# First column pair of a SwiGLU block: operand sums by halves, the order of casts and bank copies, and the buffer of the second pair's weights

## The chip, the cores and the metric

The kernel runs on one core of one Trainium2 chip. The metric is the device time of one execution in microseconds (us), as the median of several runs. Engines are named as the profile names them: PE multiplies matrices (PEld loads its weights), DVE and ACT do elementwise work, POOL a few small things, SP issues DMAs. Each engine takes its instructions strictly in the order in which the program issues them, and semaphores hold an instruction until what it needs is there.

## The reference, cut to what matters

One residual block over a sequence of 1024 rows and 1024 features: a mixer (gated DeltaNet heads beside a short convolution), then SwiGLU with 2816 hidden columns, then a last RMSNorm. Everything is float32.

```python
for l in range(DEPTH):
    shift1, scale1, gate1, shift2, scale2, gate2 = jnp.split(mod, 6, axis=-1)
    h = rms_norm(x, norm1_w[l]) * (1.0 + scale1) + shift1
    x = x + gate1 * hybrid_mixer(h, ...)
    h = rms_norm(x, norm2_w[l]) * (1.0 + scale2) + shift2
    x = x + gate2 * swiglu(h, w_gate[l], w_up[l], w_down[l])
return rms_norm(x, norm_f_w)

def swiglu(h, w_gate, w_up, w_down):
    return (jax.nn.silu(h @ w_gate) * (h @ w_up)) @ w_down
```

The change lies where the mixer ends and the first two products of SwiGLU, `h @ w_gate` and `h @ w_up`, begin.

## The kernel before

**Stages.** The first 520 us of the profile are the mixer and its output projection. From there to 944 us PE makes `h @ w_gate` and `h @ w_up` (matmuls into tiles named `acc`), then `@ w_down` (tiles named `dn`).

**Precision.** Every operand is held as two fp32r parts: a high part `hi`, the cast of the value (on ACT), and a low part `lo`, the value less `hi` (on DVE). One product of 128x512 is three matmuls, hi·hi, hi·lo and lo·hi (line 1859). So each operand tile costs one ACT instruction and one DVE instruction, the second waiting for the first.

**Tiling.** The 2816 hidden columns are taken in 11 pairs `p` of 256 columns. For a pair, gate (q = 0) and up (q = 1) are each a product of 2x2 blocks done with seven block products instead of eight (the Winograd form of Strassen's method). `STEPS` (line 44) lists the seven steps by bank, weight operand, activation operand, and whether the bank is begun anew:

```python
STEPS = (("X", "A11", "B11", True), ("Y", "A12", "B21", True), ("X", "S2", "T2", False), ("Z", "S1", "T1", True),
         ("X", "S3", "T3", False), ("Z", "S4", "B22", False), ("X", "A22", "T4", False))
```

The A operands are blocks of the weights, S1 to S4 sums of them: S1 = A21 + A22, S2 = S1 - A11, S3 = A11 - A21, S4 = A12 - S2. The B operands are blocks of the transposed activations, T1 to T4 sums of those. `run(p, s, q_)` issues step `s`: 12 matmuls for each q, 24 for both. Before a bank is added to further, its running value is taken out: `keep` copies both q of it into a `cc` tile (ACT), `close` adds it to one (DVE).

**The first pair.** For p = 0 the T operands and B22 don't exist yet. They are made once, between the steps of the first pair, in an order written out by hand at the end of the function (from line 2094), while the steps of all later pairs come from the loop `block(p, s)`. The helpers there: `t_split(n, banks)` transposes four tiles on PE into four PSUM banks (`tr`); `t_turned(n)` makes the hi and lo parts from these banks and, for T2, then copies the four banks into the `raw` tiles `tm[k]` with ACT; `t_sums` and `t_parts` make T3 and T4 from tiles in SBUF; `part(n, q)` makes hi and lo of a weight operand; `W[0].sum_n(n)` makes a weight sum, for p = 0 as two instructions, one for each q. The four transposes of T1 use the same four banks as those of T2, so they come after the copies of T2's banks.

**Weights.** `Weights(p).load(half)` issues two DMAs of 512 KB (gate and up) into one R tile of a pool with two R buffers. That pool is opened on the room of the x tiles, after these have been read for the last time: the first buffer lies over the tiles x 0 and x 1, the second over x 2 and x 3. The last readers of these are the four instructions of `t_sums("T4")`, one for each x tile.

**Names in rows.** `hl`: hi and lo of a weight operand; `S`: a weight sum; `T` or `h` with `tr`: hi and lo of T2, T1 or B22; `raw<-tr`: the copies of T2's banks; `raw<-x,raw`: T4's sums; `x<-raw,db,x`: T3's sums; `R<-R`: S3; `R<-R,S`: S4. All rows of this part of the program have line L89 (PE) or L90 (the others), which are the lines of a helper.

Of the kernel before, what the change touches and what calls it, by code (L numbers as in the profile page):

```python
# [9 lines left out]
F32 = mybir.dt.float32  # L10
F32R = mybir.dt.float32r
BF16 = mybir.dt.bfloat16
AF = mybir.ActivationFunctionType
ALU = mybir.AluOpType
# [3 lines left out]
P = 128  # L18
# [33 lines left out]
def kernel(  # L52
# [67 lines left out]
    class Banks:  # L120
# [3 lines left out]
        def get(self, name="ps"):  # L124
            b = self.ids[self.i % len(self.ids)]
            self.i += 1
            return psp.tile([P, HT], F32, name=nm(name), tag=f"b{b}")
# [78 lines left out]
    def split(raw, hi, lo, eng, hi_eng=ACT):  # L206
        cpy(hi_eng, hi, raw)
        eng.tensor_tensor(lo, raw, hi.bitcast(F32), ALU.subtract)
# [334 lines left out]
    b2c = cst.tile([P, KB], F32, name="b2c", tag="b2c")  # L543
# [1251 lines left out]
    def t_split(n, banks):  # L1795
        for k in range(4):
            def get(k=k):
                if n == "T1":
                    return h_slot(k, 1)
                if n == "B22":  # L1800
                    return h_slot(k + 4, 1)
                return mp.tile([P, 2, HT], F32R, name=nm(n), tag=f"{n}_{k}", bufs=1)
            c0 = k * P + (HT if n == "B22" else 0)
            srcs = [tm[i][:, k * P:(k + 1) * P] if n == "T2" else
                    x2n[i + (4 if n == "B22" else 0)][:, c0:c0 + P] for i in range(4)]
            ps = bank_tile(banks[k], "tr")
            for i, src in enumerate(srcs):
                pe("pe", PE.transpose(ps[:, i * P:(i + 1) * P], src, ident))
            t_ps[n, k] = ps, get

    def t_turned(n):
        for k in range(4):
            ps, get = t_ps[n, k]
            B[n][k] = dst = get()
            hi, lo = dst[:, 0, :], dst[:, 1, :]
            if n == "T1":
                split(ps, hi, lo, DVE)
            else:
                col = b2c[:, 4 + k:5 + k]
                ACT.activation(hi, ps, AF.Identity, bias=col, scale=1.0)  # L1820
                DVE.scalar_tensor_tensor(lo, ps, col, hi.bitcast(F32), ALU.add, ALU.subtract)
        if n == "T2":
            for k in range(4):
                ACT.copy(tm[k], t_ps[n, k][0])

    t_ps = {}

    def t_sums(n):
        for k in range(4):
            if n == "T3":  # L1830
                DVE.scalar_tensor_tensor(kept[k], tm[k], db2[:, k:k + 1], kept[k], ALU.add, ALU.subtract)
            else:
                DVE.tensor_tensor(tm[k], kept[4 + k], tm[k], ALU.subtract)
# [6 lines left out]
    def part(n, q):  # L1840
        W[0].cast(n, q)
        W[0].low(n, q)
# [69 lines left out]
    def close(p, n, b):  # L1912
        for q in (0, 1):
            DVE.tensor_tensor(c[p][n][q], c[p][n][q], bk[p][q][b], ALU.add)
# [43 lines left out]
    def block(p, s):  # L1958
# [17 lines left out]
        elif s == 1:  # L1976
            if w:
                if p < 2:
                    keep(p, "p1", "X")
                w.cast("S1", 0)  # L1980
                w.cast("S1", 1)
            if p > 0:
                o = p - 1
                a11, s1, a21 = c[o]["p1"][0], c[o]["p1"][1], c[o]["u2"][0]
                DVE.tensor_tensor(a11, s1, a11, ALU.subtract)
                DVE.tensor_tensor(a21, c[o]["z5"][1], a11, ALU.subtract)
                store(o, "S2", a11)
                store(o, "S4", a21)
            if w:
                w.low("S1", 0)  # L1990
                w.low("S1", 1)
                w.sum_n("S3")
        elif s == 2:
            if p < 2:
                close(p, "p1", "Y")
            else:
                close_inner(p, "p1")
            w.cast("S3", 0)
            silu(p, "p1")
            w.cast("S3", 1)  # L2000
            w.low("S3", 0)
            w.low("S3", 1)
            act(p, "p1")
            store(p, "A11", c[p]["p1"][0])
            w.sum_n("S4")
        elif s == 3:
            keep(p, "u2", "X")
            w.mat("S4")
            prep_gate(p - 1)
        elif s == 4:  # L2010
            keep(p, "z5", "Z")
            w.mat("A22")
            prep_sums(p - 1)
            if last:
                first_mats(0, "A11", am_scr)
        elif s == 5:
            close(p, "z5", "X")
            if n:
                n.cast("A11", 0)
            silu(p, "z5")  # L2020
            if n:
                n.cast("A11", 1)
                n.low("A11", 0)
                n.low("A11", 1)
            act(p, "z5")
            store(p, "A22", c[p]["z5"][0])
            if last:
                first_mats(1, "B11", None)
        elif s == 6:
            close(p, "u2", "Z")  # L2030
            if n and p:
                n.inner_sums()
                n.inner_cast(0)
            elif n:
                n.cast("A12", 0)
            silu(p, "u2")
            if n and p:
                n.inner_cast(1)
                n.inner_low(0)
                n.inner_low(1)  # L2040
            elif n:
                n.cast("A12", 1)
                n_slot[0] += 2
                n.low("A12", 0)
                n.low("A12", 1)
            act(p, "u2")
            a11, a21, a22, s1, s3 = c[p]["p1"][0], c[p]["u2"][0], c[p]["z5"][0], c[p]["p1"][1], c[p]["u2"][1]
            DVE.tensor_tensor(s1, a21, a22, ALU.add)
            DVE.tensor_tensor(s3, a11, a21, ALU.subtract)
            store(p, "S1", s1)  # L2050
            store(p, "S3", s3)
            if n and p:
                for i in (2, 3):
                    n.inner_cast(i)
                    n.inner_low(i)
            if last:
                first_mats(2, "A12", am_scr)
# [36 lines left out]
    dma(x2_scr[7], x2[7])  # L2094
    run(0, 0)
    run(0, 1, (0,))
    W[0].sum_n("S1")
    W[0].sum_n("S2")
    keep(0, "p1", "X")
    part("S2", 0)  # L2100
    part("S2", 1)
    t_split("T2", (6, 7, 4, 5))
    t_turned("T2")
    part("S1", 0)
    run(0, 1, (1,))
    t_split("T1", (6, 7, 4, 5))
    part("S1", 1)
    t_turned("T1")
    close(0, "p1", "Y")
    run(0, 2)  # L2110
    t_sums("T3")
# [4 lines left out]
    t_parts("T3")  # L2116
    run(0, 3, (0,))
    part("S3", 1)
    t_sums("T4")
    W[0].sum_n("S4")  # L2120
    t_split("B22", (6, 7, 2, 3))
    part("S4", 0)
    t_turned("B22")
    x2_ctx.__exit__(None, None, None)
    xq_ctx = tc.tile_pool(name="xq", bufs=1, side="right", reuse_waits="tile")
    xq = xq_ctx.__enter__()
    W[1] = Weights(1)
    W[1].load(0)
    W[1].load(1)
# [2 lines left out]
    run(0, 4)  # L2132
    part("S4", 1)
    part("A22", 0)
    t_parts("T4")
    part("A22", 1)
    act(0, "p1")
# [244 lines left out]
```

## Time and profile before

| | us |
|---|---|
| median of 3 runs (lowest, highest) | 1160.85 (1160.6, 1161.65) |
| the profiled execution, its own time | 1163.06 |
| its span, from the first to the last instruction | 1161.1 |
| mixer and output projection, to the first `acc` matmul of SwiGLU | 520.2 |
| the first column pair, steps 0 to 6 | 520.2 to 566.9 |
| the other ten pairs | 566.9 to 944 |
| `@ w_down` and the last norm | 944 to 1161 |

The span is the time between the first and last instruction of one profiled execution; its own time has 2 us more around it. A timeline row gives start, length, engine, line, operation, output and inputs with their size, the number of merged instructions, and in brackets the idle time before them with what ended it. A merged row's length runs to the end of its last instruction, and consecutive matmuls overlap, so how long a group took on PE is read from its start to the next group's start.

### The profile page before, as it was taken

To read this page: it belongs to the slowest core of one execution; us is meant where nothing else is said; L and a number is where in the kernel's file an instruction comes from. 1 tells how busy PE (TensorE), PEld (TensorE's weight loads), DVE (VectorE), ACT (ScalarE), POOL (GpSimd) and SP (SyncE) were. 2 spreads that over 40 slices of the span, in tenths; PEclk is the share of its full clock that TensorE was granted. 3 is DMA by queue.
4 is the path that set the end of the run, shared out by engine and by line. 5 is a ranking of instruction groups with operands and counts; after the bars stand their busy time and mean duration, and the time that the engine had idled before them with its cause. 6 is when DMAs were issued, how large, how long until landed. Compare 5 with 4: busy or idle time off the path is not lost.

```text
span 1161.1 us, 16878 instructions
## 1 busy us (share of the span) xinstructions
PE 1149.2 (99%) x5682; PEld 967.1 (83%) x5682; DVE 957.9 (83%) x1807; ACT 571.5 (49%) x1257; POOL 59.5 (5%) x100
## 2 busy tenths in 40 slices
PE   9999999999999999999999999999999999999997
PEld 7888888888888888888788888888888888888886
DVE  7899889899987898668987779777887798688676
ACT  7779633459634552445534443434434465443344
POOL 2110001002101010100000000000000000000002
PEclk9999999999999999999999999999999999999999
DMA  9823455534225455432464456545654599869403
GB/s 360 325 90 103 146 164 152 181 119 148 96 67 172 155 189 172 184 100 63 164 217 148 153 191 217 176 136 179 235 187 142 176 331 392 310 207 339 143 31 145
DMA packets 127542, 209.18 MB, mean 180 GB/s; under 512 B 20576, under 2 KB 45152, under 8 KB 127456
## 3 DMA queue, kind: packets, MB, share of 16 engines
q1 hardware_dynamic: 122080, 204.90, 51.5%
q10 hardware_dynamic: 5376, 3.21, 0.9%
q8 instruction: 45, 0.74, 0.2%
q14 instruction: 41, 0.34, 0.1%
HBM read 153.01 MB, written 55.05 MB: 179 GB/s over the span
## 4 chain that ended last, share of the span: by engine, by line
PE 90%; DVE 4%; ACT 2%; DMA 2%; issue 1%; ACTq 0%; SPq 0%; POOL 0%; DVEq 0%
PE acc L89 33%; PE acc L448 25%; PE dn L89 17%; PE o L448 4%; PE o L89 1%; PE A L448 1%; PE K L448 1%; DMA R<-in_w_up_dram 1%; DVE xo L90 1%; PE ab L448 1%; PE O L448 1%; PE kk L448 1%; DVE x L90 1%; DVE h L90 1%; ACT hl L90 0%
## 5 line engine op out<-in xcount | busy, mean ns | idle before, releaser
L448 PE MATMUL acc<-h,u 128*128 128x512 f32 x1200 | 298.6, 397 | 0.0
L448 PEld LDWEIGHTS acc<-h,u 128*128 128x128 f32 x1200 | 219.4, 188 | 42.4 <-issue 0.5
L89 PE MATMUL acc<-h,hl 128*128 128x512 f32 x576 | 135.3, 390 | 0.9 <-ACT cc L90 0.9
L89 PE MATMUL acc<-T,hl 128*128 128x512 f32 x552 | 130.9, 390 | 0.9 <-DVE cc L90 0.9
L89 PEld LDWEIGHTS acc<-h,hl 128*128 128x128 f32 x576 | 107.3, 188 | 23.2 <-ACT cc L90 1.3
L89 PEld LDWEIGHTS acc<-T,hl 128*128 128x128 f32 x552 | 102.3, 188 | 21.7 <-issue 1.3
L90 DVE TENSOR_TENSOR xo<-xo,dn 128x512 f32<-128x512 f32 x84 | 57.0, 683 | 42.3 <-PE dn L89 34.5
L89 PE MATMUL acc<-h,u 128*128 128x512 f32 (+1 forms) x480 | 91.8, 341 | 0.0
L89 PE MATMUL dn<-h,h 128*128 128x512 f32 x396 | 90.7, 389 | 0.0
L89 PEld LDWEIGHTS acc<-h,u 128*128 128x128 f32 x480 | 78.3, 189 | 11.7
L89 PEld LDWEIGHTS dn<-h,h 128*128 128x128 f32 x396 | 74.3, 188 | 15.4
L448 ACT CAST u<-raw 128x512 fp32r<-128x512 f32 x66 | 40.6, 620 | 63.8 <-PE acc L448 60.4
L90 DVE TENSOR_TENSOR cc<-cc,acc 128x512 f32<-128x512 f32 x66 | 41.4, 645 | 32.6 <-PE acc L89 32.6
L448 DVE TENSOR_TENSOR u<-raw,u 128x512 fp32r<-128x512 f32 x82 | 56.1, 686 | 9.1 <-ACT u L448 8.8
L89 PE MATMUL acc<-T,u 128*128 128x512 f32 x240 | 56.0, 389 | 0.0
L448 DVE SCALAR_TENSOR_TENSOR cv<-pr,cols_a,cv 128x512 f32<-128x512 f32 x72 | 53.4, 747 | 0.9 <-ACT cv L448 0.5
L90 ACT CAST hl<-S 128x512 fp32r<-128x512 f32 x44 | 25.3, 624 | 58.1 <-DVE S L90 58.1
L90 ACT ACTIVATE cc<-cc 128x512 f32<-128x512 f32 x33 | 20.9, 632 | 65.6 <-DVE cc L90 65.6
L90 ACT CAST h<-rw 128x512 fp32r<-128x512 f32 x57 | 32.7, 618 | 41.1 <-PE dn L89 34.6
L89 PEld LDWEIGHTS acc<-T,u 128*128 128x128 f32 x240 | 45.1, 188 | 9.3
L90 DVE TENSOR_TENSOR hl<-S,hl 128x512 fp32r<-128x512 f32 x44 | 28.4, 688 | 27.8 <-ACT hl L90 27.7
L90 ACT CAST u<-R 128x512 fp32r<-128x512 f32 (+1 forms) x60 | 34.2, 585 | 34.4 <-DVE R L90 34.2
(377 smaller groups left out, 2136.1 us busy)
## 6 DMA issues: line engine op xcount, KB each, us to landing
raw<-in_w_in_dram SPq DMA_DIRECT2D x82, 256.0 KB, 3.1
am_scr<-cc SPq DMA_DIRECT2D x77, 256.0 KB, 4.3
raw<-in_w_ada_dram SPq DMA_DIRECT2D x56, 256.0 KB, 3.3
rw<-am_scr SPq DMA_DIRECT2D x55, 256.0 KB, 5.2
rw<-bm_scr SPq DMA_DIRECT2D x53, 256.0 KB, 5.3
bm_scr<-raw SPq DMA_DIRECT2D x51, 256.0 KB, 5.4
R<-in_w_gate_dram SPq DMA_DIRECT2D x22, 512.0 KB, 4.0
R<-in_w_up_dram SPq DMA_DIRECT2D x22, 512.0 KB, 5.3
```

The costliest lines, as they stand in the source:

```text
L89: return call(*a, **k)
L90: ins = call(*a, **k)
L448: ins = call(*a, **k)
```

## The change

1. `t_turned` becomes three functions. `t_high` makes the four hi parts (ACT), `t_low` the four lo parts (DVE), `t_raw` copies T2's four banks, two with ACT and two with DVE (before, all four with ACT).
2. S1 and S2 of the first pair are summed q by q: S1 and S2 of q = 0, then of q = 1. Before: S1 of both, then S2 of both.
3. The order written out by hand changes around T2, T1 and B22: T2's hi and lo parts come between the two halves of S2; S1's first half comes after T1's transposes; B22's hi parts come ahead of S4's first cast; T4's sums come after B22's lo parts instead of ahead of S4's sums.
4. `close(0, "z5", "X")` moves out of `block` (for p = 0 alone) to a place ahead of T4's parts.
5. An R tile `R0` is allocated in the weights' pool ahead of the second pair's weights, and nothing uses it.

```python
    xq.tile([P, 2, 4, 2, P], F32, name="R0", tag="R", bufs=2)
```

In the built program the two R tiles of the second pair lie at the same addresses before and after, the first over x 0 and x 1, the second over x 2 and x 3. PE's order of work is the same in both.

```diff
--- before.py
+++ after.py
@@ -1808,20 +1808,26 @@
                 pe("pe", PE.transpose(ps[:, i * P:(i + 1) * P], src, ident))
             t_ps[n, k] = ps, get
 
-    def t_turned(n):
+    def t_high(n):
         for k in range(4):
             ps, get = t_ps[n, k]
-            B[n][k] = dst = get()
-            hi, lo = dst[:, 0, :], dst[:, 1, :]
+            B[n][k] = get()
             if n == "T1":
-                split(ps, hi, lo, DVE)
+                ACT.copy(B[n][k][:, 0, :], ps)
             else:
-                col = b2c[:, 4 + k:5 + k]
-                ACT.activation(hi, ps, AF.Identity, bias=col, scale=1.0)
-                DVE.scalar_tensor_tensor(lo, ps, col, hi.bitcast(F32), ALU.add, ALU.subtract)
-        if n == "T2":
-            for k in range(4):
-                ACT.copy(tm[k], t_ps[n, k][0])
+                ACT.activation(B[n][k][:, 0, :], ps, AF.Identity, bias=b2c[:, 4 + k:5 + k], scale=1.0)
+
+    def t_low(n):
+        for k in range(4):
+            ps, (hi, lo) = t_ps[n, k][0], (B[n][k][:, 0, :], B[n][k][:, 1, :])
+            if n == "T1":
+                DVE.tensor_tensor(lo, ps, hi.bitcast(F32), ALU.subtract)
+            else:
+                DVE.scalar_tensor_tensor(lo, ps, b2c[:, 4 + k:5 + k], hi.bitcast(F32), ALU.add, ALU.subtract)
+
+    def t_raw(n):
+        for k in range(4):
+            (ACT.copy if k < 2 else DVE.tensor_copy)(tm[k], t_ps[n, k][0])
 
     t_ps = {}
 
@@ -2014,7 +2020,8 @@
             if last:
                 first_mats(0, "A11", am_scr)
         elif s == 5:
-            close(p, "z5", "X")
+            if p:
+                close(p, "z5", "X")
             if n:
                 n.cast("A11", 0)
             silu(p, "z5")
@@ -2094,18 +2101,22 @@
     dma(x2_scr[7], x2[7])
     run(0, 0)
     run(0, 1, (0,))
-    W[0].sum_n("S1")
-    W[0].sum_n("S2")
+    for q in (0, 1):
+        W[0].sum_n("S1", (q,))
+        W[0].sum_n("S2", (q,))
     keep(0, "p1", "X")
     part("S2", 0)
+    t_split("T2", (6, 7, 4, 5))
+    t_high("T2")
+    t_low("T2")
     part("S2", 1)
-    t_split("T2", (6, 7, 4, 5))
-    t_turned("T2")
-    part("S1", 0)
+    t_raw("T2")
     run(0, 1, (1,))
     t_split("T1", (6, 7, 4, 5))
+    part("S1", 0)
     part("S1", 1)
-    t_turned("T1")
+    t_high("T1")
+    t_low("T1")
     close(0, "p1", "Y")
     run(0, 2)
     t_sums("T3")
@@ -2116,14 +2127,16 @@
     t_parts("T3")
     run(0, 3, (0,))
     part("S3", 1)
-    t_sums("T4")
     W[0].sum_n("S4")
     t_split("B22", (6, 7, 2, 3))
+    t_high("B22")
     part("S4", 0)
-    t_turned("B22")
+    t_low("B22")
+    t_sums("T4")
     x2_ctx.__exit__(None, None, None)
     xq_ctx = tc.tile_pool(name="xq", bufs=1, side="right", reuse_waits="tile")
     xq = xq_ctx.__enter__()
+    xq.tile([P, 2, 4, 2, P], F32, name="R0", tag="R", bufs=2)
     W[1] = Weights(1)
     W[1].load(0)
     W[1].load(1)
@@ -2132,6 +2145,7 @@
     run(0, 4)
     part("S4", 1)
     part("A22", 0)
+    close(0, "z5", "X")
     t_parts("T4")
     part("A22", 1)
     act(0, "p1")
```

Three places in the order of instructions, of the kernel before and of the changed one.

**DVE, the first pair, from S1's sum on.** S_5494 is S1; S_5497 before and S_5496 after are S2; hl_5504 is the lo part of S2 for q = 0, hl_5507 before and hl_5539 after that for q = 1; the rows with tr are T2's lo parts. Before:

```order
L90 TENSOR_TENSOR S_5494<-R_5445,R_5449 128x512
L90 TENSOR_TENSOR S_5494<-R_5446,R_5450 128x512
L90 TENSOR_TENSOR S_5497<-S_5494,R_5445 128x512
L90 TENSOR_TENSOR S_5497<-S_5494,R_5446 128x512
L90 TENSOR_TENSOR hl_5504<-S_5497,hl_5504 128x512
L90 TENSOR_TENSOR hl_5507<-S_5497,hl_5507 128x512
L90 SCALAR_TENSOR_TENSOR T_1002_5530<-tr_5510,b2c,T_1002_5530 128x512
L90 SCALAR_TENSOR_TENSOR T_1003_5533<-tr_5515,b2c,T_1003_5533 128x512
L90 SCALAR_TENSOR_TENSOR T_1004_5536<-tr_5520,b2c,T_1004_5536 128x512
L90 SCALAR_TENSOR_TENSOR T_1005_5539<-tr_5525,b2c,T_1005_5539 128x512
L90 TENSOR_TENSOR hl_5546<-S_5494,hl_5546 128x512
```

After:

```order
L90 TENSOR_TENSOR S_5494<-R_5445,R_5449 128x512
L90 TENSOR_TENSOR S_5496<-S_5494,R_5445 128x512
L90 TENSOR_TENSOR S_5494<-R_5446,R_5450 128x512
L90 TENSOR_TENSOR S_5496<-S_5494,R_5446 128x512
L90 TENSOR_TENSOR hl_5504<-S_5496,hl_5504 128x512
L90 SCALAR_TENSOR_TENSOR T_1001_5527<-tr_5507,b2c,T_1001_5527 128x512
L90 SCALAR_TENSOR_TENSOR T_1002_5529<-tr_5512,b2c,T_1002_5529 128x512
L90 SCALAR_TENSOR_TENSOR T_1003_5531<-tr_5517,b2c,T_1003_5531 128x512
L90 SCALAR_TENSOR_TENSOR T_1004_5533<-tr_5522,b2c,T_1004_5533 128x512
L90 TENSOR_TENSOR hl_5539<-S_5496,hl_5539 128x512
L90 COPY raw_5395<-tr_5517 128x512
L90 COPY raw_5437<-tr_5522 128x512
```

S2 of q = 0 no longer stands behind the second sum of S1; the lo part of S2 for q = 1 stands behind T2's; and two copies of T2's banks (the COPY rows) now stand in DVE's order, ahead of S1's lo parts.

**DVE and ACT, from T4's sums or S4's sums on.** The rows `raw<-x,raw` are T4's sums, R_5449 and R_5450 become S4, the rows with tr are B22's lo parts. DVE before:

```order
L90 TENSOR_TENSOR raw_5246<-x_0_4583,raw_5246 128x512
L90 TENSOR_TENSOR raw_5314<-x_1_4584,raw_5314 128x512
L90 TENSOR_TENSOR raw_5395<-x_2_4585,raw_5395 128x512
L90 TENSOR_TENSOR raw_5437<-x_3_4586,raw_5437 128x512
L90 TENSOR_TENSOR R_5449<-R_5449,S_5497 128x4x128
L90 TENSOR_TENSOR R_5450<-R_5450,S_5497 128x4x128
L90 TENSOR_TENSOR hl_5690<-R_5449,hl_5690 128x512
L90 SCALAR_TENSOR_TENSOR h_1_1030_5693<-tr_5670,b2c,h_1_1030_5693 128x512
L90 SCALAR_TENSOR_TENSOR h_1_1031_5696<-tr_5675,b2c,h_1_1031_5696 128x512
L90 SCALAR_TENSOR_TENSOR h_1_1032_5699<-tr_5680,b2c,h_1_1032_5699 128x512
L90 SCALAR_TENSOR_TENSOR h_1_1033_5702<-tr_5685,b2c,h_1_1033_5702 128x512
L90 TENSOR_TENSOR hl_5754<-R_5450,hl_5754 128x512
```

DVE after:

```order
L90 TENSOR_TENSOR R_5449<-R_5449,S_5496 128x4x128
L90 TENSOR_TENSOR R_5450<-R_5450,S_5496 128x4x128
L90 TENSOR_TENSOR hl_5694<-R_5449,hl_5694 128x512
L90 SCALAR_TENSOR_TENSOR h_1_1029_5686<-tr_5666,b2c,h_1_1029_5686 128x512
L90 SCALAR_TENSOR_TENSOR h_1_1030_5688<-tr_5671,b2c,h_1_1030_5688 128x512
L90 SCALAR_TENSOR_TENSOR h_1_1031_5690<-tr_5676,b2c,h_1_1031_5690 128x512
L90 SCALAR_TENSOR_TENSOR h_1_1032_5692<-tr_5681,b2c,h_1_1032_5692 128x512
L90 TENSOR_TENSOR raw_5246<-x_0_4583,raw_5246 128x512
L90 TENSOR_TENSOR raw_5314<-x_1_4584,raw_5314 128x512
L90 TENSOR_TENSOR raw_5395<-x_2_4585,raw_5395 128x512
L90 TENSOR_TENSOR raw_5437<-x_3_4586,raw_5437 128x512
L90 TENSOR_TENSOR hl_5755<-R_5450,hl_5755 128x512
```

T4's four sums stood ahead of S4's sums and now stand behind B22's lo parts. On ACT, hl_5690 before and hl_5694 after are S4's hi part for q = 0, and cc_5727 before and cc_5728 after take bank Z out (`keep(0, "z5", "Z")`). ACT before:

```order
L90 CAST hl_5661<-R_5446 128x512
L90 CAST hl_5690<-R_5449 128x512
L90 ACTIVATE h_1_1030_5693<-tr_5670,b2c 128x512
L90 ACTIVATE h_1_1031_5696<-tr_5675,b2c 128x512
L90 ACTIVATE h_1_1032_5699<-tr_5680,b2c 128x512
L90 ACTIVATE h_1_1033_5702<-tr_5685,b2c 128x512
L90 COPY cc_5727<-acc_5647 128x512
L90 COPY cc_5727<-acc_5648 128x512
```

ACT after:

```order
L90 CAST hl_5661<-R_5446 128x512
L90 ACTIVATE h_1_1029_5686<-tr_5666,b2c 128x512
L90 ACTIVATE h_1_1030_5688<-tr_5671,b2c 128x512
L90 ACTIVATE h_1_1031_5690<-tr_5676,b2c 128x512
L90 ACTIVATE h_1_1032_5692<-tr_5681,b2c 128x512
L90 CAST hl_5694<-R_5449 128x512
L90 COPY cc_5728<-acc_5647 128x512
L90 COPY cc_5728<-acc_5648 128x512
```

S4's first cast, which waits for DVE's sum, stood ahead of B22's four hi parts and of the two copies out of bank Z; now it stands behind the hi parts.

**DVE, the end of the first pair.** The rows `cc_5727<-cc_5727,acc` before and `cc_5728<-cc_5728,acc` after are `close(0, "z5", "X")`, the rows `T<-raw,T` T4's lo parts. Before:

```order
L90 TENSOR_TENSOR hl_5757<-R_5449,hl_5757 128x512
L90 TENSOR_TENSOR T_1039_5760<-raw_5246,T_1039_5760 128x512
L90 TENSOR_TENSOR T_1040_5763<-raw_5314,T_1040_5763 128x512
L90 TENSOR_TENSOR T_1041_5766<-raw_5395,T_1041_5766 128x512
L90 TENSOR_TENSOR T_1042_5769<-raw_5437,T_1042_5769 128x512
L90 TENSOR_TENSOR hl_5772<-R_5450,hl_5772 128x512
L90 TENSOR_TENSOR cc_5500<-cc_5501,cc_5500 128x512
L90 TENSOR_TENSOR cc_5727<-cc_5727,acc_5454 128x512
L90 TENSOR_TENSOR cc_5727<-cc_5727,acc_5455 128x512
```

After:

```order
L90 TENSOR_TENSOR hl_5758<-R_5449,hl_5758 128x512
L90 TENSOR_TENSOR cc_5728<-cc_5728,acc_5454 128x512
L90 TENSOR_TENSOR cc_5728<-cc_5728,acc_5455 128x512
L90 TENSOR_TENSOR T_1039_5763<-raw_5246,T_1039_5763 128x512
L90 TENSOR_TENSOR T_1040_5766<-raw_5314,T_1040_5766 128x512
L90 TENSOR_TENSOR T_1041_5769<-raw_5395,T_1041_5769 128x512
L90 TENSOR_TENSOR T_1042_5772<-raw_5437,T_1042_5772 128x512
L90 TENSOR_TENSOR hl_5775<-R_5450,hl_5775 128x512
L90 TENSOR_TENSOR cc_5500<-cc_5501,cc_5500 128x512
```

The two additions that take bank X out stood behind T4's four lo parts, A22's last lo part (hl_5772) and one product; now they stand ahead of T4's lo parts.

## The prediction

> **What bounds the kernel now.** First the page's table of busy times, then the busy time of each engine by stretch (start and end, length, then busy time with the number of instructions; the last columns are the granted clock, the share of the DMA engines, GB/s).
>
> ```profile
> PE 1149.2 (99%) x5682; PEld 967.1 (83%) x5682; DVE 957.9 (83%) x1807; ACT 571.5 (49%) x1257; POOL 59.5 (5%) x100
> 528.40:567.00 38.60, 36.29 (x182) 29.69 (x181) 36.19 (x59) 24.76 (x46) 0.00 (x0) 1.00 0.30 96
> 567.00:944.00 377.00, 377.00 (x1841) 319.54 (x1840) 308.36 (x494) 154.54 (x299) 0.00 (x0) 1.00 0.53 181
> 944.00:1147.00 203.00, 203.00 (x897) 167.96 (x896) 153.73 (x247) 90.48 (x171) 5.94 (x16) 1.00 0.68 241
> ```
>
> PE sets the time almost everywhere; from 567 to 1147 it never idles. In the first pair it does, and there DVE is the busy one: 36.19 of 38.60 us. The chain that ended last says the same: in the first pair it runs through DVE and ACT, and from 561.38 on through PE alone.
>
> ```profile
> 528.17 1.30 DVE S L90 x2
> 550.50 0.61 DVE R L90
> 554.09 1.09 ACT cc L90 x2
> 561.38 383.34 PE acc L89 x1866
> ```
>
> So the change can win what PE loses here, and a gain here shifts everything behind it. PE's timeline shows where it loses:
>
> ```profile
> 528.41 1.91 PE L89 MATMUL tr<-ident,raw 128*128 128x128 f32 x16
> 530.08 2.98 PE L89 MATMUL acc<-h,hl 128*128 128x512 f32 x12
> 533.57 2.12 PE L89 MATMUL tr<-ident,x 128*128 128x128 f32 x16 [0.51 <-ACT raw L90]
> 535.44 5.72 PE L89 MATMUL acc<-T,hl 128*128 128x512 f32 x24
> 541.00 2.89 PE L89 MATMUL acc<-h,hl 128*128 128x512 f32 x12
> 545.39 3.02 PE L89 MATMUL acc<-h,hl 128*128 128x512 f32 x12
> 548.24 5.60 PE L89 MATMUL acc<-T,hl 128*128 128x512 f32 x24
> 554.74 5.74 PE L89 MATMUL acc<-h,hl 128*128 128x512 f32 x24 [0.90 <-ACT cc L90]
> 561.38 5.72 PE L89 MATMUL acc<-T,hl 128*128 128x512 f32 x24 [0.90 <-DVE cc L90]
> 566.94 5.60 PE L89 MATMUL acc<-h,hl 128*128 128x512 f32 x24
> 572.38 5.60 PE L89 MATMUL acc<-h,u 128*128 128x512 f32 x24
> ```
>
> The pace is the last row's start less the one before: 24 matmuls in 5.44, so 12 in 2.72. Sixteen transposes take 530.08 - 528.41 = 1.67, and 12 matmuls behind transposes 548.24 - 545.39 = 2.85. Against that, start to start: the 12 at 530.08 take 3.49, 0.64 too long; T1's transposes 1.87, 0.20 too long; step 4 (at 548.24) 6.50, 1.06 too long; step 5 (554.74) 6.64, 1.20 too long; step 6 (561.38) 5.56, 0.12 too long. Together 3.22 us, which is all that can be won here. The idle time that the same rows show is only 0.51 + 0.90 + 0.90 = 2.31, since the modelled ends of matmuls overlap and the restart is slow.
>
> The Trainium skill (Trainium Kernel Development and Optimization, Performance Expectations) says that matmul busy time is a bad measure, because matmuls are pipelined. By busy time the whole sum would be capped at 2.31, a time of 1158.5; the pace in the rows bears out the rule, and the sum here goes by the pace.
>
> **The change part by part.** The rows of DVE, ACT and SP on which it rests:
>
> ```profile
> 528.17 0.69 DVE L90 TENSOR_TENSOR S<-R,R 128x512 f32<-128x512 f32 x1 [1.38 <-DMA R<-in_w_up_dram]
> 528.78 1.29 DVE L90 TENSOR_TENSOR S<-S,R 128x512 f32<-128x512 f32 x2
> 531.36 2.72 DVE L90 SCALAR_TENSOR_TENSOR T<-tr,b2c,T 128x512 fp32r<-128x512 f32 x4
> 535.53 1.29 DVE L90 TENSOR_TENSOR hl<-S,hl 128x512 fp32r<-128x512 f32 x2 [1.45 <-ACT hl L90]
> 547.41 0.69 DVE L90 TENSOR_TENSOR hl<-R,hl 128x512 fp32r<-128x512 f32 x1
> 548.01 2.49 DVE L90 TENSOR_TENSOR raw<-x,raw 128x512 f32<-128x512 f32 x4
> 550.42 1.29 DVE L90 TENSOR_TENSOR R<-R,S 128x512 f32<-128x512 f32 x2
> 560.55 1.27 DVE L90 TENSOR_TENSOR cc<-cc,acc 128x512 f32<-128x512 f32 x2
> 532.91 2.06 ACT L90 COPY raw<-tr 128x512 f32<-128x512 f32 x4
> 534.81 1.20 ACT L90 CAST hl<-S 128x512 fp32r<-128x512 f32 x2
> 551.27 0.62 ACT L90 CAST hl<-R 128x512 fp32r<-128x512 f32 x1 [4.30 <-PE acc L89]
> 551.80 2.42 ACT L90 ACTIVATE h<-tr,b2c 128x512 fp32r<-128x512 f32 x4
> 554.09 1.09 ACT L90 COPY cc<-acc 128x512 f32<-128x512 f32 x2
> ```
>
> Steps from start to start: a DVE sum or lo part 0.60 (four in 550.42 - 548.01), a DVE lo part with bias 0.66 (2.72 less the last one's 0.74, by three), an ACT copy of a bank 0.48 ((2.06 - 0.62) / 3), an ACT hi part with bias 0.57, an ACT cast 0.52. A lo part ends 0.69 after its start.
>
> *T2 and T1.* Nothing earlier is touched, and DVE still can't make S1's second half before the up weights land, at 528.17. Before, S2 of q = 0 and its cast queue behind that; now they run in the 1.38 us of idle time. From 528.17 DVE has S1 and S2 of q = 1 (1.21), S2's lo part (0.60), T2's four lo parts (2.64), S2's other lo part (0.60), then two copies. Its ACT partners are in time: T2's hi parts can start once the transposes of 528.41 are through, about 529.05, and run 0.57 apart, S2's second cast ends at 532.0 and ACT's two bank copies at about 533.0. So DVE's first copy starts at 528.17 + 5.05 = 533.2 and the second at 533.8.
>
> What does a DVE copy of a whole bank cost? This stage has none; a single one stands far ahead, and the next instruction starts 0.60 after it:
>
> ```profile
> 56.31 0.68 DVE L448 COPY pr<-acc 128x512 f32<-128x512 f32 x1
> 56.91 0.75 DVE L448 SCALAR_TENSOR_TENSOR cv<-pr,cols_a,cv 128x512 f32<-128x512 f32 x1
> ```
>
> The copies end at about 533.9 and 534.5. T1's transposes can start at 530.08 + 2.85 = 532.93 instead of 533.57; their third group, due at 533.77, waits 0.2 for the first copy, the fourth 0.2 more for the second. They end at 535.0 instead of 535.44: **0.44 won**, 0.4 left lying. Bounds: 0.84 if the copies are early, nothing if they come 0.4 late, by half the step of each more.
>
> The Trainium skill (VectorE: DVE Perf Modes, The TRN2 errata) lists 120 + FD cycles at 0.96 GHz for VectorE from PSUM and 172 + FD at 1.2 GHz for ScalarE: for 512 elements 0.66 and 0.57 us, which speaks against moving two copies to VectorE. By it and by the rows above (0.60 against 0.48 a step) all four on ScalarE would be done by 534.2, and the sum would be 0.3 to 0.4 better.
>
> *S4, B22 and step 5.* Before, step 5 waits for the copies out of bank Z at 554.09; these queue on ACT behind the cast of S4 at 551.27, and this behind S4's sum at 550.42, which stands behind T4's four sums. Now S1's lo parts start on DVE behind the second copy, at 534.4 instead of 535.53: the two copies cost less than the 1.45 of waiting that is gone. From there to the lo part at 547.41 the order is the same, so that comes 1.1 earlier, at 546.3, S4's sums at 546.9 and 547.5. ACT, whose casts there follow DVE's sums and so come 1.1 earlier too, makes B22's hi parts from 545.8 to 548.1, S4's cast to 548.7, the copies out of bank Z to 549.7. Step 5 would start at 553.2 (548.24 - 0.44 + 5.44): the wait is gone with 3.5 us to spare. **1.06 won** ahead of step 5, and with it the slow restart behind the wait, 0.12 as in step 6. New is a wait of DVE: the lo part of S4 for q = 0 waits for the cast until 548.75, 0.6 us, and behind it queue B22's lo parts (549.35 to 552.0), T4's sums (to 554.4), the lo parts of S4 (q = 1, ends 555.1) and of A22 (q = 0). Step 5 needs S4's second lo part at 556.4, 1.3 later. So it costs nothing as long as DVE isn't 1.3 us later than this walk.
>
> *Bank X and step 6.* Before, step 6 waits at 561.38 for the first addition of 560.55, which stands behind T4's lo parts. Now the two additions start at 555.6 and 556.2, and step 6 is due at 558.7. T4's lo parts follow from 556.8, the first is done at 557.5 and needed at 558.9. **1.08 won** ahead of step 6 (step 5's 1.20 less its restart), and step 6's own 0.12.
>
> *The second pair's weights.* `R0` moves nothing: the two tiles stay over x 0 to x 3. But their loads wait for the last readers, T4's sums, and these now come 4.0 later (second sum ends 553.3, not 549.3):
>
> ```profile
> 549.36 0.37 SPq L90 DMA_DIRECT2D R<-in_w_gate_dram  x1
> 550.57 0.37 SPq L90 DMA_DIRECT2D R<-in_w_gate_dram  x1
> DMA to landing us min/median/max: 3.4/4.7/7.6
> 558.00:560.60 2.60, 2.48 (x11) 1.71 (x10) 2.60 (x6) 1.33 (x3) 0.00 (x0) 1.00 0.00 0
> ```
>
> Before, all four are in by 558.0 (no traffic after that); now by about 562. The first is needed by PE at 564.1, with a cast and a lo part (1.4) between, so it may land as late as 562.7; issued at 553.35, and with the longest landing here, 7.6, it is there by 561.0. Cost nothing; the cover is 1.7 us even then. Behind these DMAs on SP stand the store of the first pair's A11, which waits for DVE until 560 anyway, and loads behind that.
>
> *The sum.* 0.44 + 1.06 + 0.12 + 1.08 + 0.12 = 2.8 us. The profiled span of 1161.1 becomes 1158.3, its own time 1163.06 becomes 1160.3, and the median 1160.85 (the profiled execution ran 2.2 above it, a difference that the change doesn't touch) becomes **1158.05**. Bounds: 3.2 (all lost time) gives 1157.6; 2.4 (T1's transposes win nothing) 1158.5.
>
> **The rivals.**
>
> *DVE becomes the bound.* It gets 1.2 us more to do and idles for only 2.4 in the whole stretch. If it runs 2.7 us later than the walk, through waits on ACT that I have left out, step 5's second half waits 2.7 - 1.3 = 1.4, which also covers step 6; 1.4 of the 2.8 is left, a time of 1159.4. For it: waits of 1.38 and 1.45 on others stand in its rows now. Against: those are used or removed, and in the walk only one new one, of 0.6, appears.
>
> *Slower: the second pair's weights come late.* The place is the first cast of the second pair, behind which ACT and, through its lo part, DVE stand in order. It decides from a landing at 562.7; each us later is one us of PE. The gain is gone at 565.5, and at 567.8, a load of 14.4 us from issue to landing, the kernel stands 2.3 above before: 1163.2. For it: the loads go out 4 us later while PE comes there 2.8 us earlier. Against: the DMA engines are free until then, and the worst of these loads took 7.6.
>
> *It doesn't do what it says.* The weights' buffer stays where it was. If that edit was what counted, the time stays at 1160.85. Against: the three waits shown stand behind instructions that the other edits move.
>
> **How the numbers follow.** A difference of 0.2% (2.3 us) is about what can be told from no change. The forecast has a chance of 0.76, with its own range 1157.5 to 1158.7; 0.07 of that is a gain below 2.3. DVE as the bound 0.12, late weights 0.07, of which 0.05 is beyond 0.2%, no effect 0.05. Faster by over 0.2%: 0.76 - 0.07 = 0.69; slower 0.06; within 0.25. The range is 1157.4 to 1159.7: it takes in the bounds and the first rival.
>
> **What would show it.** PE's rows: T1's transposes with a wait of about 0.4 on `DVE raw`, steps 5 and 6 without idle time, step 0 of the second pair at about 564.1 instead of 566.94. SP's load of the second pair at about 553.3. DVE with a wait of 0.6 ahead of an `hl<-R`. It would be wrong if a wait of PE on DVE stands at step 5 or 6, if the second pair starts with one on ACT `hl`, or if PE idles after 567, where it doesn't now.

## The result and the profile after

| | before, us | after, us |
|---|---|---|
| median (lowest to highest), 22 runs of each | 1161.59 (1160.6 to 1162.57) | 1159.72 (1158.9 to 1160.4) |
| the profiled execution, own time | 1163.06 | 1160.25 |
| its span | 1161.1 | 1158.5 |
| first transpose of T2 to step 0 of the second pair | 38.53 | 35.53 |

The ratio is 0.9984, with an interval from 0.9977 to 0.9990: faster by 1.87 us, or 0.16%. Forecast were 2.8 us and 1158.05, with a range up to 1159.7, which the median misses by 0.02. But the two profiled executions are 2.81 us apart, as forecast, 0.94 more than the medians. That can be if the profile of before was no ordinary execution, in the first pair or ahead of it, or if most executions of the changed kernel lose something that its profile doesn't show.

PE's timeline of the kernel after, from T2's transposes to the second pair:

```profile
528.79 1.91 PE L89 MATMUL tr<-ident,raw 128*128 128x128 f32 x16
530.45 2.98 PE L89 MATMUL acc<-h,hl 128*128 128x512 f32 x12
533.27 2.17 PE L89 MATMUL tr<-ident,x 128*128 128x128 f32 x16
535.20 5.72 PE L89 MATMUL acc<-T,hl 128*128 128x512 f32 x24
548.00 5.60 PE L89 MATMUL acc<-T,hl 128*128 128x512 f32 x24
553.44 5.60 PE L89 MATMUL acc<-h,hl 128*128 128x512 f32 x24
558.88 5.60 PE L89 MATMUL acc<-T,hl 128*128 128x512 f32 x24
564.32 5.60 PE L89 MATMUL acc<-h,hl 128*128 128x512 f32 x24
```

No row has a wait in brackets any more, and the steps from 548.00 on follow each other at the pace, 5.44. Only T1's transposes still take 1.93 (535.20 - 533.27) where 1.67 is the pace. The windows of after say the same: PE is busy in all of the stretch, DVE almost in all of it.

```profile
528.79:564.32 35.53, 35.53 (x182) 29.89 (x180) 34.71 (x57) 23.37 (x43) 0.00 (x0) 1.00 0.27 84
```

In the chain of waits of after (start, length, what), the last uninterrupted stretch of PE begins with the first matmuls behind T3's and B22's transposes, where before it began only with step 6, at 561.38:

```profile
543.64 1.75 PE tr L89 x16
545.39 396.71 PE acc L89 x1926
```

The other engines' timelines of after, at the places that the prediction names:

```profile
530.14 2.73 DVE L90 SCALAR_TENSOR_TENSOR T<-tr,b2c,T 128x512 fp32r<-128x512 f32 x4 [0.16 <-ACT T L90]
533.39 1.28 DVE L90 COPY raw<-tr 128x512 f32<-128x512 f32 x2
547.07 1.28 DVE L90 TENSOR_TENSOR R<-R,S 128x512 f32<-128x512 f32 x2
548.87 0.69 DVE L90 TENSOR_TENSOR hl<-R,hl 128x512 fp32r<-128x512 f32 x1 [0.52 <-ACT hl L90]
555.73 1.28 DVE L90 TENSOR_TENSOR cc<-cc,acc 128x512 f32<-128x512 f32 x2
548.73 1.09 ACT L90 COPY cc<-acc 128x512 f32<-128x512 f32 x2
557.59 0.62 ACT L90 CAST hl<-R 128x512 fp32r<-128x512 f32 x1 [1.80 <-DMA R<-in_w_gate_dram]
553.46 0.37 SPq L90 DMA_DIRECT2D R<-in_w_gate_dram  x1
```

The walk gave S4's sums at 546.9, the wait of DVE as 0.6, the copies out of bank Z from 548.7, the additions at 555.6, the loads at 553.35, the second pair at 564.1. Each is there within 0.25 us. The late loads make ACT wait 1.80 for the first cast of the second pair, but the cast ends at 558.2, 6 us ahead of its use at 564.32.

### The profile page after: what moved, and what is told of

The parts are those of the page before. It is cut to its first block, busy times and chain, and to the rows that moved or that the text cites. A ratio compares the mean times of both kernels' runs of the same rounds, so it can differ in the third digit from the quotient of the medians.

```text
span 1158.5 us, 16876 instructions
## 1 busy us (share of the span) xinstructions
PE 1148.1 (99%) x5682; PEld 967.1 (83%) x5682; DVE 959.8 (83%) x1809; ACT 571.1 (49%) x1255; POOL 61.9 (5%) x100
## 4 chain that ended last, share of the span: by engine, by line
PE 97%; DVE 1%; ACT 1%; DMA 0%; SPq 0%; issue 0%; ACTq 0%; DVEq 0%
PE acc L89 36%; PE acc L448 26%; PE dn L89 17%; PE o L89 4%; PE o L448 4%; PE A L448 1%; PE K L448 1%; PE tr L89 1%; DVE xo L90 1%; PE ab L448 1%; PE u L448 1%; PE w L448 1%; PE kk L448 1%; PE O L448 1%; DMA raw<-in_w_ada_dram 0%; PE qk L448 0%
```

## The experiments

In all of them the stretch from T2's first transpose to step 0 of the second pair is read, in one profiled execution, since it holds every wait of PE that the edits touch. Behind it all the profiles agree: 594.0 to 594.4 us from step 0 of the second pair to the end. At the pace the stretch takes 35.21 us. The lead is the time from the landing of the last of `W[0]`'s four loads (the second half of the up weights) to T2's first transpose; it is negative where the weights land behind it.

| kernel | lead | stretch | own time |
|---|---|---|---|
| before, the profile of the prediction | 0.34 | 38.53 | 1163.06 |
| before_again | 1.69 | 37.26 | 1161.03 |
| after | 1.61 | 35.53 | 1160.25 |
| after_again | 1.81 | 35.53 | 1159.66 |
| close_late | 2.00 | 36.93 | 1161.22 |
| t4_and_cast_undone | 1.49 | 36.03 | 1160.4 |
| t4_sums_early | 1.91 | 35.53 | 1160.37 |
| cast_first | 1.84 | 35.53 | 1159.86 |
| t2_order_undone | 1.41 | 35.21 | 1159.04 |
| raw_on_act | 1.97 | 35.21 | 1159.71 |
| before_weights_just_late | 0.09 | 38.77 | 1162.33 |
| after_weights_just_late | 0.64 | 35.55 | 1158.69 |
| after_just_late_again | 0.75 | 35.54 | 1159.43 |
| t2_undone_just_late | 0.41 | 36.08 | 1160.61 |
| before_weights_late | -4.20 | 43.05 | 1166.6 |
| after_weights_late | -3.80 | 41.59 | 1165.84 |

### Both kernels once more, unchanged

> The kernel before, unchanged, profiled once more: the trace that the prediction was made from shows 3.0 us more in the first pair than the changed kernel's trace (38.5 us from T2's first transpose to step 0 of the second pair, against 35.5), while the medians differ by 1.9. Theory A (the trace of before caught an execution that waited more in the first pair than most): the stretch is shorter here, 37.2 to 37.9. Theory B (the stretch is the same in each execution, and the stages ahead of it vary): 38.3 to 38.7, with T2's first transpose off 528.4 by half a us or more.

> The changed kernel, unchanged, profiled once more and timed. Both theories: 35.4 to 35.7 us from T2's first transpose to step 0 of the second pair, since PE waits for next to nothing there. Theory C (the changed kernel loses about 1 us behind the first pair in most executions): from step 0 of the second pair to the end more than 594.8 us, where both traces so far show 594.2. Time 1.2 to 2.7 us below the kernel before.

Before, the second profile has another first pair than the first one. PE's timeline of before_again, and the DVE row that stood at 528.17 behind a wait of 1.38:

```profile
527.48 1.91 PE L89 MATMUL tr<-ident,raw 128*128 128x128 f32 x16
529.14 2.98 PE L89 MATMUL acc<-h,hl 128*128 128x512 f32 x12
531.96 1.91 PE L89 MATMUL tr<-ident,x 128*128 128x128 f32 x16
533.63 5.70 PE L89 MATMUL acc<-T,hl 128*128 128x512 f32 x24
546.37 5.60 PE L89 MATMUL acc<-T,hl 128*128 128x512 f32 x24
552.54 5.73 PE L89 MATMUL acc<-h,hl 128*128 128x512 f32 x24 [0.57 <-ACT cc L90]
559.18 5.72 PE L89 MATMUL acc<-T,hl 128*128 128x512 f32 x24 [0.91 <-DVE cc L90]
564.74 5.60 PE L89 MATMUL acc<-h,hl 128*128 128x512 f32 x24
```

```profile
525.38 1.29 DVE L90 TENSOR_TENSOR S<-R,R 128x512 f32<-128x512 f32 x2
```

S1's two sums follow each other without a wait, T1's transposes come at the pace (531.96 - 529.14 = 2.82, then 1.67), and step 4 is 0.73 too long (552.54 - 546.37 - 5.44) where the first profile had 1.06. Step 5 is 1.20 too long and step 6 0.12, as before. In all 2.05 us are lost, not 3.22. The DMA views of a stretch around the load's issue show where this comes from (KB, then us from issue to landing), first of the prediction's trace, then of before_again:

```profile
R<-in_w_up_dram SPq DMA_DIRECT2D x1, 512.0 KB, 7.6
```

```profile
R<-in_w_up_dram SPq DMA_DIRECT2D x1, 512.0 KB, 6.3
```

In the ten profiles in which this load is as in the two kernels, it takes 5.96 to 6.54 us nine times and 7.61 once: in the profile that the prediction was made from. From 3 to 5 us behind its issue the DMA engines moved 213 GB/s there (523.46 to 525.46) and 300 in before_again (522.52 to 524.52); what slowed them stays open.

After_again agrees with after to 0.01 us in the stretch, and theory C is out: from step 0 of the second pair to the end it takes 594.3 us, not over 594.8. So by these profiles the changed kernel loses nothing behind the first pair, and the profile of before is the one out of the ordinary, in the first pair itself. The 11 timed runs of after_again have a median of 1159.56 against 1161.71 (21 runs) of before, a ratio of 0.998 (0.9971 to 0.9989).

### The landing made late on purpose

In the first try two whole stores of 512 KB stand ahead of the second half's loads; the second of them writes the same values again.

```diff
-    for half in (0, 1):
-        W[0].load(half)
-    dma(x2_scr[7], x2[7])
+    W[0].load(0)
+    for _ in range(2):
+        dma(x2_scr[7], x2[7])
+    W[0].load(1)
```

> The kernel before with two stores of x2_7 (512 KB each, the second a repetition) ahead of the loads of W[0]'s second half, so that the last of these lands about 2 us later than in most traces, where it lands 1.5 to 2 us ahead of T2's first transpose. Theory A (what PE loses in the first pair before the change depends on when these weights land): T1's transposes wait for ACT raw, and the stretch from T2's first transpose to step 0 of the second pair is 38.3 to 39.9, against 37.26 in the second trace of before. Rival (the stretch's 38.53 in the first trace came from somewhere else): 37.2 to 37.6.

> The changed kernel with the same two stores ahead of the loads of W[0]'s second half. Theory A: it loses less than the kernel before, as S2's first half and T2's parts no longer stand behind the late half: 35.6 to 37.3 where the changed kernel has 35.53, and the difference between the two late kernels is 2.4 to 2.9, not 1.7. Rival: the difference is the same 1.7 as with weights in time.

This overshot and was a miss: DVE's second sum of S1 starts 4.29 us behind T2's first transpose before, 3.90 after. The stretches are 43.05 and 41.59, a difference of only 1.46. PE waited so long there that its clock fell, which is in the last section, so the pair says nothing of the two orders at the landings that occur by themselves.

In the second try a piece of 32 KB of that store goes ahead, and the whole store follows the loads as usual. The same edit was made in both kernels:

```diff
-    for half in (0, 1):
-        W[0].load(half)
+    W[0].load(0)
+    dma(x2_scr[7][:, 0:64], x2[7][:, 0:64])
+    W[0].load(1)
     dma(x2_scr[7], x2[7])
```

> A 32 KB piece of x2 7's store goes ahead of W[0]'s second half, so that those loads wait for DVE's x2 7 and land later, here aimed at about T2's first transpose, without the long waits that slowed the clock in the runs with two whole stores. Theory (the gain of the first pair depends on when these loads land): with a landing 0.3 us ahead of T2's first transpose the stretch from that transpose to the second pair is 38.3 to 38.8; with 1.0 ahead about 37.8; with 0.7 behind 39.0 to 39.6. Rival (the landing does not matter, 38.53 against 37.26 was chance elsewhere): 37.3 whatever the landing.

> The same piece of a store ahead of W[0]'s second half in the changed kernel. Theory: with a landing 0.3 us ahead of T2's first transpose the stretch is 35.6 to 36.0, with 1.0 ahead 35.5, with 0.7 behind 36.6 to 36.9, so that the difference to the kernel before with the same piece is 2.3 to 2.9, as the prediction had it, where loads in time gave 1.7. Rival: the difference stays at 1.7.

PE and DVE of before_weights_just_late:

```profile
527.42 1.91 PE L89 MATMUL tr<-ident,raw 128*128 128x128 f32 x16
529.08 2.98 PE L89 MATMUL acc<-h,hl 128*128 128x512 f32 x12
532.83 2.12 PE L89 MATMUL tr<-ident,x 128*128 128x128 f32 x16 [0.76 <-ACT raw L90]
534.70 5.72 PE L89 MATMUL acc<-T,hl 128*128 128x512 f32 x24
554.00 5.74 PE L89 MATMUL acc<-h,hl 128*128 128x512 f32 x24 [0.90 <-ACT cc L90]
560.63 5.72 PE L89 MATMUL acc<-T,hl 128*128 128x512 f32 x24 [0.90 <-DVE cc L90]
566.20 5.15 PE L89 MATMUL acc<-h,hl 128*128 128x512 f32 x22
```

```profile
527.42 0.69 DVE L90 TENSOR_TENSOR S<-R,R 128x512 f32<-128x512 f32 x1 [1.19 <-DMA R<-in_w_up_dram]
```

This is the prediction's profile again: the wait on `ACT raw` at T1's transposes and the longer wait at step 5 are back, at a stretch of 38.77. The rival, which had 37.3 whatever the landing, is out. In the changed kernel the same edit gave a lead of 0.64, and DVE waits at the same place:

```profile
526.76 0.69 DVE L90 TENSOR_TENSOR S<-R,R 128x512 f32<-128x512 f32 x1 [0.31 <-DMA R<-in_w_up_dram]
```

but its stretch stays at 35.55, and T1's transposes begin without a wait:

```profile
531.79 2.19 PE L89 MATMUL tr<-ident,x 128*128 128x128 f32 x16
533.74 5.72 PE L89 MATMUL acc<-T,hl 128*128 128x512 f32 x24
```

The difference of the pair is 3.22; it flatters the change, since the leads aren't equal. To see how much of that the order at T2 and T1 holds, this part alone was put back in the changed kernel (the edit is shown under t2_order_undone below) together with the piece of a store; and the changed kernel ran once more.

> The changed kernel with the order of S1, S2, T2, T1 and the four ACT copies as before, and the 32 KB piece of x2 7's store ahead of W[0]'s second half. With loads in time this order had a stretch of 35.21, 0.32 better than the changed one. Theory (the edits at T2 and T1 pay only when the loads land late): with a landing 0.1 to 0.3 ahead of T2's first transpose T1's transposes wait again, 0.7 to 1.1 us, and the stretch is 36.0 to 36.4; with 0.6 ahead 35.6 to 35.9; so the term of the prediction, 0.44, or more of it, is there. Rival (those edits are worth nothing in any case): stretch 35.2 to 35.3, T1's transposes without a wait.

> The changed kernel with the piece of a store ahead of W[0]'s second half once more, since its first run had these loads 0.64 ahead of T2's first transpose and the kernel before 0.09. Theory: 35.5 to 35.6 with a lead of 0.6 or more, 35.6 to 36.0 with 0.1 to 0.3. Rival (the changed order doesn't absorb a late landing): 36.5 or more at a lead of 0.1 to 0.3.

PE of t2_undone_just_late:

```profile
533.42 2.12 PE L89 MATMUL tr<-ident,x 128*128 128x128 f32 x16 [0.45 <-ACT raw L90]
```

With the old order and a lead of 0.41 the wait at T1's transposes is there, and the stretch is 36.08; with the new order, at leads of 0.64 and 0.75, it is 35.55 and 35.54. The difference of 0.53 flatters the new order, as its loads came earlier. In the kernel before, each us of lead is worth about one us of the stretch (38.53 at 0.34, 38.77 at 0.09), so at a lead of 0.64 the old order would have about 35.85, an estimate, and the edits at T2 and T1 be worth about 0.3 there. How the new order fares at a lead of 0.1 to 0.4 was not measured: the loads of both its runs came earlier than aimed.

### The edits one by one, with the weights in time

The additions to bank X back at their old place:

```diff
         elif s == 5:
-            if p:
-                close(p, "z5", "X")
+            close(p, "z5", "X")
...
-    close(0, "z5", "X")
     t_parts("T4")
```

> The changed kernel with the additions that take bank X out (the close of z5) back behind T4's lo parts. If these additions are what step 6 waited for before: step 6 waits 1.1 to 1.5 us for DVE cc again, and the stretch from T2's first transpose to step 0 of the second pair is 36.7 to 37.2. Rival (DVE's earlier start alone had ended that wait): no wait, 35.5.

```profile
559.50 5.72 PE L89 MATMUL acc<-T,hl 128*128 128x512 f32 x24 [1.11 <-DVE cc L90]
```

PE's row of step 6 in close_late: the wait is back, and the stretch is 36.93, 1.40 more than after. Of the 1.73 between before_again and after, this one edit makes most.

T4's sums and S4's first cast both back at their old places:

```diff
+    t_sums("T4")
     W[0].sum_n("S4")
     t_split("B22", (6, 7, 2, 3))
-    t_high("B22")
     part("S4", 0)
+    t_high("B22")
     t_low("B22")
-    t_sums("T4")
```

> The changed kernel with T4's sums ahead of S4's sums and S4's first cast ahead of B22's hi parts, as before. By the walk the copies out of bank Z then come about 0.5 late for step 5: a wait there on ACT cc, stretch 35.9 to 36.2. The prediction gave 1.06 and a restart to these edits together: 36.7.

```profile
553.09 5.75 PE L89 MATMUL acc<-h,hl 128*128 128x512 f32 x24 [0.20 <-ACT cc L90]
```

Step 5 waits again for the copies out of bank Z, and the stretch is 36.03: 0.50 for the two together. Each half of that edit alone:

> The changed kernel with T4's four sums ahead of S4's again; B22's high parts stay ahead of S4's first cast. Theory (either of the two edits is enough to have bank Z copied in time; both undone cost 0.50): stretch 35.5, no wait of PE at step 5, and the second pair's loads go out at about 549 again, which changes nothing. Rival (T4's sums are what counted): the wait of 0.5 to 0.6 at step 5 comes back, stretch 36.0.

> The changed kernel with S4's first cast ahead of B22's high parts on ACT again; T4's sums stay behind. Theory: stretch 35.5, no wait at step 5. Rival (the order on ACT is what counted): a wait of 0.5 to 0.6 at step 5, stretch 36.0.

Both have a stretch of 35.53, as after. ACT's rows of the copies out of bank Z, first in t4_sums_early, then in cast_first:

```profile
550.84 1.07 ACT L90 COPY cc<-acc 128x512 f32<-128x512 f32 x2
```

```profile
549.98 1.09 ACT L90 COPY cc<-acc 128x512 f32<-128x512 f32 x2
```

Step 5 begins at 553.56 and 552.69 there, at the pace. Either order is enough, and the second pair's loads, which t4_sums_early issues at 548.54 again, don't matter for the stretch.

The order of S1, S2, T2 and T1 and the four copies on ACT as before, alone:

```diff
-            (ACT.copy if k < 2 else DVE.tensor_copy)(tm[k], t_ps[n, k][0])
+            ACT.copy(tm[k], t_ps[n, k][0])
...
-    for q in (0, 1):
-        W[0].sum_n("S1", (q,))
-        W[0].sum_n("S2", (q,))
+    W[0].sum_n("S1")
+    W[0].sum_n("S2")
     keep(0, "p1", "X")
     part("S2", 0)
+    part("S2", 1)
     t_split("T2", (6, 7, 4, 5))
     t_high("T2")
     t_low("T2")
-    part("S2", 1)
     t_raw("T2")
+    part("S1", 0)
     run(0, 1, (1,))
     t_split("T1", (6, 7, 4, 5))
-    part("S1", 0)
     part("S1", 1)
```

> The changed kernel with the order of before from S1's sum to T1's transposes (sums not by halves, both halves of S2 ahead of T2, T2's four bank copies on ACT, S1's first half ahead of T1's transposes); the edits around B22, T4 and bank X stay. If theory A holds and the weights land in time, this part of the change wins nothing and costs what its two DVE copies cost: 35.1 to 35.3, 0.3 below the changed kernel. By the prediction, which gave this part 0.44 of its 2.8: 35.9 to 36.1.

And only the first line of that edit, the four copies on ACT, with everything else as changed:

> The changed kernel with all four copies of T2's banks on ACT again. By the prediction's walk the copies are done by 534 instead of 534.5, T1's transposes no longer wait, and the stretch from T2's first transpose to step 0 of the second pair is 0.4 us shorter than the changed kernel's: 35.0 to 35.2. Rival: ACT, busy with S1's and T1's casts, is late with these, and step 3 waits: 35.5 or more.

Both reach 35.21. T1's transposes take 1.67 again, here in t2_order_undone (533.73 - 532.07, to rounding):

```profile
532.07 1.91 PE L89 MATMUL tr<-ident,x 128*128 128x128 f32 x16
533.73 5.70 PE L89 MATMUL acc<-T,hl 128*128 128x512 f32 x24
```

So with the weights in time the two copies on DVE are what costs 0.32 in the changed kernel, and the rest of the reordering at T2 and T1 wins nothing. In the times this can't be seen: raw_on_act has a median of 1159.78 in 11 runs, a ratio to before of 0.9984 (0.9975 to 0.9993), after_again of 1159.56 in the same round. No version ran that is shown to beat the changed kernel.

## Why the prediction was wrong by 1.7 us

**The waits at steps 5 and 6 and their causes were right.** These steps were held up by the instructions named, the edits took the waits away, and T4's later sums and loads cost nothing. That the walk of DVE and ACT came out within 0.25 us is in part luck: T2's transposes began at 528.79 in after, not at the 528.41 of the walk, and the weights landed 1.27 earlier against them. Counted from T2's first transpose, the walk is 0.16 (second pair) to 0.35 us (copies out of bank Z) too late.

**What failed** is the step "the profiled execution ran 2.2 above it, a difference that the change doesn't touch", and with it "DVE still can't make S1's second half before the up weights land, at 528.17", which took one landing for the landing. Of those 2.2 us, 38.53 - 37.26 = 1.27 lay in the very stretch that the change touches, and were made by the transfer of 7.6 us that the prediction had quoted as the longest of its kind: before_weights_just_late brings them back with a late landing alone. In the nine other profiles with these loads unchanged the weights land 1.4 to 2.0 us ahead of T2's transposes, and neither before_again nor after waits for them. By these profiles the late landing is the rare case; how often it occurs in the timed runs isn't known. The match of the forecast 2.8 with the 2.81 between the two profiled executions is chance too: in the stretch they are 3.00 us apart, 1.27 of them from that one landing, and the rest of the two executions gives 0.19 back.

The terms, by the profiles with the weights in time (before_again and after):

| term | predicted | measured | how |
|---|---|---|---|
| T2 and T1 | +0.44 | -0.32 | 0 lost before, 0.32 after |
| S4, B22, step 5 | +1.06 | +0.73 | step 4 of before_again, 0 after |
| bank X, step 6, restarts | +1.32 | +1.32 | 1.20 + 0.12 of before_again, 0 after |
| sum | 2.82 | 1.73 | |

So 0.76 of the miss is the first term, 0.33 the second. The other part is the base: the three runs shown had a median of 1160.85, 0.74 below that of 22 runs. 1158.05 + 0.76 + 0.33 + 0.74 = 1159.88, and 1159.72 was measured; the 0.16 between them is unexplained. The single edits undone give 1.40 + 0.50 - 0.32 = 1.58 in place of 1.73; the edits act on one another's waits, so they need not add up.

**The first term's own size.** In the profiles with late weights its mechanism holds (36.08 against 35.55, at unequal leads), and the two DVE copies leave T1's transposes behind the pace as forecast, by 0.26 us with the weights in time and 0.28 at a lead of 0.64, where the forecast had 0.4. In all eight profiles with these two copies and no long wait of PE, T1's transposes take 1.92 to 1.95 us instead of 1.67; the reordering pays only where the weights come late. The durations weighed there (the Trainium skill, VectorE: DVE Perf Modes, The TRN2 errata), longer for VectorE than for ScalarE, spoke for all four copies on ScalarE. The prediction's estimate from them and its rows was 0.3 to 0.4 better; raw_on_act agrees, with 0.32 in the stretch.

**The rivals.** DVE becoming the bound would have given about the time that was measured, 1159.4, but it is not the cause: no wait of PE on DVE is left at step 5 or 6, and at T1's transposes DVE holds PE up by 0.26 alone. Late weights of the second pair: not there. No effect: excluded by the interval; with 22 runs of each kernel it tells 1.87 us from nothing, where the prediction took 2.3 for about the least that can be told. A median that came out between forecast and rival would have passed for the first rival, had the profile not been taken again.

## What to carry to other kernels

When a profiled execution lies above all timed runs, find where its extra time lies before subtracting it as a constant: if it is in the stretch that the change touches, part of the forecast gain is that execution's own. A wait of an engine on a DMA is a draw from a spread of landing times (5.96 to 7.61 us for one load here), so its term of the sum should be worked out for the usual landing as well as for the one in the trace. Once a kernel stands at the pace of its bounding engine, a reordering should be undone piece by piece: of four edits here, one made most of the gain, two did the same work, and one, the two copies moved to DVE, cost 0.32 with the weights in time.

## What the runs showed of the hardware

A wait of PE that is long enough costs more than itself. In before, waits of 0.90 us left the granted clock at 1.00. In the runs with two whole stores PE waits 5.05 us, and 2.60 + 0.68 us:

```profile
537.30 3.68 PE L89 MATMUL tr<-ident,x 128*128 128x128 f32 x16 [5.05 <-ACT raw L90]
540.63 6.09 PE L89 MATMUL acc<-T,hl 128*128 128x512 f32 x24
```

```profile
535.63 1.97 PE L89 MATMUL tr<-ident,x 128*128 128x128 f32 x8 [2.60 <-ACT raw L90]
538.28 1.94 PE L89 MATMUL tr<-ident,x 128*128 128x128 f32 x8 [0.68 <-DVE raw L90]
```

The first two rows are before_weights_late, the other two after_weights_late. Sixteen transposes take 3.33 us (540.63 - 537.30) instead of 1.67. The windows (the granted clock is the third number from the end), in the same order of kernels:

```profile
534.00:534.50 0.50, 0.00 (x0) 0.00 (x0) 0.50 (x2) 0.50 (x2) 0.00 (x0) 1.00 0.00 0
534.50:535.00 0.50, 0.00 (x0) 0.00 (x0) 0.50 (x2) 0.50 (x2) 0.00 (x0) 0.57 0.00 0
541.00:541.50 0.50, 0.50 (x2) 0.39 (x2) 0.50 (x2) 0.50 (x2) 0.00 (x0) 0.61 0.00 0
```

```profile
535.00:535.30 0.30, 0.00 (x0) 0.00 (x0) 0.30 (x1) 0.30 (x1) 0.00 (x0) 0.86 0.00 0
542.00:542.50 0.50, 0.50 (x3) 0.41 (x3) 0.50 (x2) 0.00 (x0) 0.00 (x0) 0.96 0.00 0
```

A window's mean between 1.00 and 0.50 dates the switch: at 0.57 the clock fell 0.07 us into the window of 534.50. So it fell to 0.50 at 534.57 and came back at about 541.39 in the one, at about 535.22 and 542.04 in the other: 6.82 us at half clock in both, from a point some 2.2 to 2.3 us into the wait. The Trainium skill (TensorE: Matmul & The Clock Gate, What's actually happening) has the clock go to half after an idle window of about 3.4 us and back after a busy one as long, in windows that run free of the kernel. By that figure two such windows are 6.8 us, an estimate, and the 6.82 measured agree; that 2.2 to 2.3 us of idleness were enough does not agree with a whole idle window. At the end of the two kernels the clock falls once more, at 1162.62 and 1159.86 (0.72 in the window 1162.40 to 1162.90, 0.76 in 1159.60 to 1160.10). That is 621.23 and 617.82 us after it came back, 182 and 181 times 3.413, and 6.82 is twice that. So in these two runs the switches lie on a grid of 3.413 us, and in the last 3.41 us ahead of the falls at 534.57 and 535.22 PE had still worked for over 1 us.

In the changed kernel more of the half clock fell on work, since its wait was shorter: from 535.63 to 542.04, less the wait of 0.68, which is 5.73 us, against 4.09 from 537.30 to 541.39. Half of each is lost, so the changed kernel lost about 0.8 more to the clock, an estimate; at an equal loss the difference of the pair would have been about 2.3 instead of 1.46.
